# A decoder block in one core: up weights' low parts by an adding DMA, RNN work spread, one product moved

## The chip, the cores and the metric

The kernel runs on one core of one Trainium2 chip. The metric is the device time of an execution in microseconds (us). The core has a matrix engine (TensorE, PE in the rows; its weight loads are PEld), a vector engine (VectorE, DVE), an activation engine (ScalarE, ACT), a general engine (GpSimd, POOL) and a queue that issues transfers (SyncE, SP). Sixteen DMA engines move data between memory (HBM) and the on-chip memory (SBUF). TensorE accumulates in eight PSUM banks of 128 x 512 floats. Its clock has two levels, 2.4 and 1.2 GHz; the rows give the granted clock as a share of the higher one.

## What is computed

One decoder block over 512 tokens of width 1024, all in float32: a sparse attention with a top-k index, and a gated linear recurrence (RG-LRU), merged; then a convolutional feed-forward part. Cut to what matters here:

```
h  = cumulative recurrence of (a, x * i * sqrt(1 - a^2)) over the tokens   # 1024 channels
rnn = h * gelu(yr)
q, k, v, qi, ki, ... = split(rms_norm(x) @ w_in)       # attention over the 128 keys of best index score
h  = x + ga1 * (merge(attention, rnn) @ w_out)
up = causal_conv3(rms_norm(h) @ w_up)                  # 1024 -> 2 x 2816
val, gte = split(up)
h  = h + ga2 * ((silu(gte) * val) @ w_down)            # 2816 -> 1024
return rms_norm(h)
```

## The kernel before

**Three products for one.** Every float32 operand of a large product is split into a high part, rounded to the type that TensorE multiplies at full rate (fp32r), and a low part, the rest. A product is then three matmuls: high x high, high x low, low x high (`mm3`). For weights `split` (line 550) makes them: ScalarE copies the raw tile into the high part `wh`, VectorE subtracts that from the raw tile into the low part `wl`. `wtile` (line 755) loads the raw weights, one 1 MB DMA for two tiles of 128 output columns, and calls `split`.

**A planner sets the order.** The code records operations in `Plan.op` (line 199) with a planned cost, the engines that may run it, and its buffers; `Plan.order` (line 241) then simulates the engines, picks operations by a due time (`rank`) and writes out one fixed order for each engine. `P.fix` gives TensorE's work its planned time, `P.soft` gives an operation a due time, `P.hor` says how long before its due time it may take a buffer (`HORIZON` for most). Buffers are rings: `W` three raw weight tiles of 1 MB, `w` six split tiles, thus three pairs of high and low part, `t` 75 tiles of 128 x 512, `b` eight PSUM banks. In hardware each engine runs its list in order, so what waits holds up what stands behind it.

**The stages.** First the input projections by tiles (`xr`, `yr`, `qi`, `kw`, `k`, `v`, `q`, the gates). In between run the recurrent branch in two batches of four 128-channel blocks (`rnn_batch`, line 820), the index scores and the top-k loops on VectorE, and the attention. In `rnn_batch` the last part does for each block `m = sqrt(m)`, `u = u * m`, the scan `h`, `y = gelu(y)` and `y = y * h`; the due times are `at(RB[3])` and `at(RB[4])`, the same for all four blocks. Then come the output projections and the norm of the second half.

**The feed-forward part.** 44 up tiles follow (`up`, line 1213; tiles 2f and 2f+1 are the value and gate half of f tile f, 22 of them). An up tile is 8 x 3 matmuls of 512 columns. ScalarE takes its bank out into `cv`, VectorE adds two more convolution taps, and after each second tile comes the SiLU and the product with the other half, `acts[f]`. The down projection of f tiles 0 to 15 is done by one level of Strassen: seven products in place of eight (`product`, line 1177), each once over pairs 0 to 3 and once over pairs 4 to 7; the second round of seven is placed behind the up tiles named in `SPREAD[1]`, and each product's two banks are added into `total`. F tiles 16 to 21 go the plain way in the tail (line 1269 on): for every row block of 128 tokens (`ROWS` = 2, 3, 0, 1) and half of the columns six f tiles of three matmuls into one bank, then sum, norm and output. Their split weights are `dh`, `dl`, their split activations `acth`, `actl`.

Of the kernel before, what the change touches and what calls it, by code (L numbers as in the profile page):

```python
# [19 lines left out]
TT = S // 128  # L20
# [23 lines left out]
INFLATE = 1.03  # L44
HORIZON = 26
EARLY = 3
PAIRS = 8
ORDER = [[4, 3, 0, 2, 1, 5, 6], [0, 1, 2, 3, 4, 5, 6]]
ROWS = [2, 3, 0, 1]
SLICES = [(0, 4), (4, 8)]  # L50
SPREAD = [[17, 19, 21, 23, 25, 27, 29], [32, 34, 36, 37, 39, 41, 42]]
OUTS = [("wr", (0, 1, 2, 3)), ("wa", (0, 1)), ("wr", (4, 5)), ("wa", (2, 3, 4, 5, 6, 7)), ("wr", (6, 7))]
ADA0 = 28
COLD = 8.0
RBIAS = [14.0, 46.0, 48.0]
WARM = 12
DOT1 = 13.24
SECOND = -23.6
LATER = 13.94
CLOCK = 9.79  # L60
RB = [3.28, 6.04, 7.96, 11.0, 13.85, 0.61]
SOON = [20.91, 19.0, 21.69, 11.19]
ISTEP = {1: 14.0, 2: 38.5, 3: 93.3}
IW = {1: 18, 2: 49.4, 3: 51.9}
ASTEP = {0: 76, 1: 99.0, 2: 126, 3: 145}
AW = [8.6, 6.1, 18.7, 30.4]
BUMP = [0.01, 0.81]

# [96 lines left out]
class Op:  # L165
    __slots__ = ("engs", "emit", "reads", "writes", "deps", "succ", "rank", "idx", "func", "ready", "left",
                 "fixed", "soft", "hor", "after", "weak", "allocs", "lat", "end", "bufs", "start", "eng", "n", "tag", "shares")

# [8 lines left out]
class Plan:  # L177
# [20 lines left out]

    def op(self, engs, reads, writes, emit, func=None, hold=(), n=1, tag="", follow=None):
        o = Op()  # L200
        o.engs, o.emit, o.func = engs, emit, func
        o.n, o.tag = n, tag
# [38 lines left out]
    def order(self):  # L241
        ops = self.ops
        for o in reversed(ops):
            cost = min(o.engs.values())
            late = 1e9
            for s in o.succ:
                late = min(late, s.rank - 0.25 - cost * INFLATE)
            if o.fixed is not None:
                late = o.fixed
            if o.soft is not None:  # L250
                late = min(late, o.soft)
            o.rank = late
# [91 lines left out]
        while len(out) < n:  # L344
# [37 lines left out]
            for b in o.bufs:  # L382
                b.left -= 1
                b.end = max(b.end, o.end)
                if b.left == 0 and b.kind in SLOTS:
                    frees[b.kind].append(b.end + 0.1)
            for s in o.succ:
                s.left -= 1
                s.ready = max(s.ready, t if o in s.weak else o.end + max(LAT[e][x] for x in s.engs))
                if s.left == 0:  # L390
                    for x in s.engs:
                        avail[x].append(s)
# [7 lines left out]
def block_kernel(ctx: ExitStack, tc: tile.TileContext, x, cols, wada1, wada2, win0, win, wgate,  # L400
# [13 lines left out]
    def buf(kind, shape, dtype, name, reserve=0):  # L414
        uid[0] += 1
        return Buf(kind, shape, dtype, f"{name}_{uid[0]}", reserve)
# [338 lines left out]
    def wtile(src, c, sub, nk):  # L755
        key = (id(src), c)
        if key not in raws:
            raws[key] = buf("W", (128, nk, 256), F32, "wr")
            dma(raws[key], src[c], 128 * nk * 256 * 4)
        hi, lo = buf("w", (128, nk, 128), F32R, "wh"), buf("w", (128, nk, 128), F32R, "wl")  # L760
        split(hi, lo, raws[key][:, :, sub * 128:(sub + 1) * 128])
        return hi, lo
# [57 lines left out]
    def rnn_batch(js):  # L820
# [19 lines left out]
        for j in js:  # L840
# [9 lines left out]
            am[j] = (a, m)  # L850
        for j in js:
            a, m = am[j]
            u = g[j, 1]
            at(RB[3])
            act(m, m, AF.Sqrt)
            tt(u, u, m, ALU.mult, ("dve", "pool"))
            h = t2(name="h")
# [3 lines left out]
            at(RB[4])  # L861
            act(y, y, AF.Gelu_apprx_tanh)
            tt(y, y, h, ALU.mult, ("dve", "pool"))
            P.soft, P.hor = None, 20.0
# [403 lines left out]

    full = slice(0, 512)
    for t in ROWS:  # L1270
        parts, outs = [], []
        c = slice(t * 128, (t + 1) * 128)
        for h in range(2):
            cut = (t, h) == (ROWS[-1], 1)
            for n in [slice(0, 256), slice(256, 512)] if cut else [full]:
                ps = bank()
                for f in range(tail, FT):
                    hi, lo = dsplit[f, h]
                    planned(3 * pass_us(n.stop - n.start))
                    mm3(ps[:, n], asplit[f][0][:, c], asplit[f][1][:, c], hi[:, n], lo[:, n], f == tail, f == FT - 1)  # L1280
                    P.fix = None
                P.soft = clock[0] + 1.0
                v = total[t, h][:, n]
                tt(v, ps[:, n], v, ALU.add)
                o = t2(name="o")
                parts.append(v)
                outs.append((o, n, h))
                P.soft = clock[0] + 2.5
                tt(o[:, n], v, gfin[h][:, n], ALU.mult)
                P.soft = None  # L1290
        P.soft = clock[0] + 1.0
# [52 lines left out]
def _layout(i):  # L1344
# [25 lines left out]
    o["w_out"] = i["w_out"][0].reshape(4, 2, 128, 1024).transpose(0, 2, 1, 3)  # L1370
    o["w_up"] = _chunk(i["w_up"][0][:, ffo], 256)
    o["w_down"] = i["w_down"][0].reshape(11, 2, 128, 1024).transpose(0, 2, 1, 3)
# [26 lines left out]
```

## Time and profile before

| | |
|---|---|
| time, median of 3 runs | 787.84 us (786.66 to 787.93) |
| the profiled execution's own time | 790.1 us |
| its span, first to last instruction | 788.3 us |
| TensorE busy, matmuls | 768.4 us, 3579 |
| VectorE busy | 666.9 us |
| ScalarE busy | 461.4 us |
| GpSimd busy | 50.5 us |
| moved by the DMA queues | 126.22 MB |
| mean granted TensorE clock | 0.992 |

Busy time of TensorE is modelled from starts: matmuls overlap, so the distance between two starts says more than the length of one. "Idle before" is time in which the engine did nothing, with what ended it behind an arrow. Of a DMA the issue is seen on the queue of the engine that issues it, and its landing as the time until its semaphore.

### The profile page before, as it was taken

Reading aid. Unit: us, or ns where it says so; the run is one execution under the profiler, and the core shown is the slowest. Engines: PE = TensorE matmul, PEld = TensorE weight load, DVE = VectorE, ACT = ScalarE, POOL = GpSimd, SP = SyncE. Lnnn points to the kernel's source line nnn. Section 1 sums busy time; section 2 is a strip of 40 time slices with the busy share of each in tenths; the row PEclk is TensorE's granted clock in tenths of the full one; section 3 lists DMA queues with packets and bytes.
Section 4 is the critical chain, followed back from the end, with each engine's and each line's share of the span. In section 5 each row is a group of like instructions: output and inputs, shape, how many; then the busy total and the mean of one; then the engine's idle time right before and its main releaser. Section 6 shows DMA issues by size and latency. Waiting matters only on the chain.

```text
span 788.3 us, 10204 instructions
## 1 busy us (share of the span) xinstructions
PE 768.4 (97%) x3579; PEld 639.7 (81%) x3579; DVE 666.9 (85%) x1315; ACT 461.4 (59%) x815; POOL 50.5 (6%) x72
## 2 busy tenths in 40 slices
PE   7999999999899999999999999999999999999986
PEld 6888888887788887888789988888888888888865
DVE  6996976999999988869885867897977889997973
ACT  6589935599599779723335643665534454443522
POOL 1000000034021141000000000000000000000000
PEclk9999999999899999999999999999999999999999
DMA  9973132231121351648671343456445544676202
GB/s 342 404 276 111 54 128 85 81 133 54 54 107 55 133 187 55 223 163 312 242 274 39 134 178 116 160 193 209 160 160 199 176 178 155 217 247 201 98 27 81
DMA packets 35411, 126.22 MB, mean 160 GB/s; under 512 B 3944, under 2 KB 6432, under 8 KB 25504
## 3 DMA queue, kind: packets, MB, share of 16 engines
q1 hardware_dynamic: 35360, 125.58, 44.8%
q8 instruction: 28, 0.46, 0.2%
q14 instruction: 23, 0.19, 0.1%
HBM read 121.35 MB, written 5.79 MB: 161 GB/s over the span
## 4 chain that ended last, share of the span: by engine, by line
PE 54%; DVE 24%; DMA 12%; issue 4%; ACT 4%; SPq 0%; POOLq 0%; POOL 0%; DVEq 0%; ACTq 0%
PE ps L534 53%; DMA wd<-in_w_down_dram 7%; DVE dl L470 3%; DMA wr<-in_w_up_dram 3%; DVE wl L470 3%; DVE sum L470 3%; DVE cv L475 2%; DVE wd L470 2%; DVE wa L621 2%; DMA wa<-in_wada_dram 2%; PE ps L546 2%; ACT wh L463 1%; DMA wo<-in_w_out_dram 1%; DVE ahl L470 1%; DVE sc L901 1%
## 5 line engine op out<-in xcount | busy, mean ns | idle before, releaser
L534 PE MATMUL ps<-yl,wh 128*128 128x512 f32 (+1 forms) x376 | 141.7, 377 | 0.1
L534 PE MATMUL ps<-yh,wh 128*128 128x512 f32 (+1 forms) x376 | 141.4, 376 | 0.0
L534 PE MATMUL ps<-yh,wl 128*128 128x512 f32 (+1 forms) x376 | 141.2, 375 | 0.0
L463 ACT ACTIVATE wh<-wr 128x1024 fp32r<-128x1024 f32 (+1 forms) x96 | 97.7, 1019 | 59.6 <-PE ps L534 40.9
L470 DVE TENSOR_TENSOR wl<-wr,wh 128x1024 fp32r<-128x1024 f32 (+1 forms) x96 | 112.9, 1176 | 17.5 <-ACT wh L463 17.1
L534 PE MATMUL ps<-xh,wh 128*128 128x512 f32 x288 | 114.0, 396 | 0.0
L534 PE MATMUL ps<-xh,wl 128*128 128x512 f32 x288 | 113.2, 393 | 0.4 <-DVE wl L470 0.4
L534 PE MATMUL ps<-xl,wh 128*128 128x512 f32 x288 | 113.1, 393 | 0.0
L463 ACT ACTIVATE dh<-wd 128x512 fp32r<-128x512 f32 x68 | 42.5, 630 | 78.0 <-DVE wd L470 69.9
L534 PEld LDWEIGHTS ps<-yl,wh 128*128 128x128 f32 x376 | 70.7, 188 | 13.3 <-DVE yl L470 0.5
L534 PEld LDWEIGHTS ps<-yh,wl 128*128 128x128 f32 x376 | 70.7, 188 | 12.9
L534 PEld LDWEIGHTS ps<-yh,wh 128*128 128x128 f32 x376 | 70.7, 188 | 12.8
L475 DVE SCALAR_TENSOR_TENSOR cv<-ps,ct,cv 128x511 f32<-128x511 f32 x88 | 65.6, 745 | 11.9 <-ACT cv L463 11.2
L534 PE MATMUL ps<-dh,ahl 128*128 128x512 f32 x224 | 71.3, 389 | 0.0
L534 PEld LDWEIGHTS ps<-xh,wl 128*128 128x128 f32 x288 | 54.6, 189 | 12.7 <-DVE wl L470 1.2
L534 PEld LDWEIGHTS ps<-xl,wh 128*128 128x128 f32 x288 | 54.7, 190 | 10.3
L534 PEld LDWEIGHTS ps<-xh,wh 128*128 128x128 f32 x288 | 54.7, 190 | 10.2
L621 DVE SCALAR_TENSOR_TENSOR wa<-wa,crow 128x1024 f32<-128x1024 f32 x48 | 58.5, 1235 | 2.2 <-DMA wa<-in_wada_dram 2.2
L534 PEld LDWEIGHTS ps<-dh,ahl 128*128 128x128 f32 x224 | 42.0, 188 | 8.7
L470 DVE TENSOR_TENSOR dl<-wd,dh 128x512 fp32r<-128x512 f32 x68 | 45.8, 684 | 3.4 <-ACT dh L463 3.1
L463 ACT ACTIVATE cv<-ps,ct 128x512 f32<-128x512 f32 x44 | 33.7, 766 | 17.9 <-PE ps L534 17.9
L534 PE MATMUL ps<-dl,ahl 128*128 128x512 f32 x112 | 43.6, 389 | 0.0
(256 smaller groups left out, 1483.9 us busy)
## 6 DMA issues: line engine op xcount, KB each, us to landing
wa<-in_wada_dram SPq DMA_DIRECT2D x24, 1024.0 KB, 4.8
wd<-in_w_down_dram SPq DMA_DIRECT2D x96, 256.0 KB, 3.4
wr<-in_w_up_dram SPq DMA_DIRECT2D x22, 1024.0 KB, 5.0
wr<-in_win_dram SPq DMA_DIRECT2D x18, 1024.0 KB, 4.8
wr<-in_wo_rnn_dram SPq DMA_DIRECT2D x4, 1024.0 KB, 4.7
wo<-in_w_out_dram SPq DMA_DIRECT2D x4, 1024.0 KB, 4.9
wd<-in_w_down_dram SPq DMA_DIRECT2D x3, 1024.0 KB, 4.9
x<-in_x_dram SPq DMA_DIRECT2D x4, 512.0 KB, 9.6
```

The source lines that it names most:

```text
L463: nc.scalar.activation(real(dst), real(src), func, **kw)
L470: lambda e: ENG[e].tensor_tensor(real(dst), real(a), real(b), op=op), tag="tt")
L475: lambda e: nc.vector.scalar_tensor_tensor(real(dst), real(a), real(s), real(b), op0=op0, op1=op1), tag="stt")
L534: nc.tensor.matmul(real(ps), real(a), real(b), start=st, stop=sp)
L546: nc.tensor.transpose(real(ps[:, i * 128:(i + 1) * 128]), real(s), real(ident))
L621: vop(1.14, [r, crow], [r, dst], lambda: nc.vector.scalar_tensor_tensor(real(r), real(r), 1.0, real(crow), op0=ALU.mult, op1=ALU.mult, acc ...
L901: vop(0.125 + 0.00104 * W, [a, m8], [a], lambda m8=m8: nc.vector.match_replace(real(a), real(m8), real(a), TAKEN))
```

## The change

It has four parts.

1. In `wtile`, for up tiles from number 6 on (38 of the 44), the low part is no longer made by VectorE. ScalarE writes the high part, and in a second pass, with scale -1, the negated high part into the buffer of the low part. Then a DMA issued by GpSimd reads the raw weights of that tile once more from memory and adds them to it. The planner gives it 1.0 us on GpSimd and 3.0 us more until its result is there (`extra`). The layout of `w_up` in memory changes so that a tile's 512 KB are 4 KB a partition in one piece; the 1 MB load of two tiles stays.
2. In `rnn_batch` the u x m products and scans, and the y x h products, have due times of their own: a start (14.0 us behind the first batch's base, 24.7 behind the second's) plus 9.1 or 10.0 us for each further block, and 3.0 more for y x h.
3. The second round of products is placed behind other up tiles, the last one behind tile 43, the last of all, in place of tile 42. In the tail the first row block does f tiles 16 to 19 for both halves before f tiles 20 and 21.
4. The planner's constants: `HORIZON` 41 in place of 26, costs of ScalarE, VectorE and GpSimd 5% higher, and other due times.

```diff
-HORIZON = 26
+HORIZON = 41
+FIRST = 6
-SPREAD = [[17, 19, 21, 23, 25, 27, 29], [32, 34, 36, 37, 39, 41, 42]]
+SPREAD = [[17, 19, 21, 23, 25, 27, 28], [32, 33, 36, 38, 39, 42, 43]]
+SLACK = {"act": 1.05, "dve": 1.05, "pool": 1.05}
-DOT1 = 13.24
-SECOND = -23.6
-LATER = 13.94
-CLOCK = 9.79
-RB = [3.28, 6.04, 7.96, 11.0, 13.85, 0.61]
-SOON = [20.91, 19.0, 21.69, 11.19]
-ISTEP = {1: 14.0, 2: 38.5, 3: 93.3}
-IW = {1: 18, 2: 49.4, 3: 51.9}
-ASTEP = {0: 76, 1: 99.0, 2: 126, 3: 145}
-AW = [8.6, 6.1, 18.7, 30.4]
-BUMP = [0.01, 0.81]
+DOT1 = 14.92
+SECOND = -21.2
+LATER = 8.59
+CLOCK = 9.89
+RB = [3.28, 6.04, 7.96, 11.0, 15.86, 0.61]
+RNNV = [[14.0, 9.1], [24.7, 10.0]]
+SOON = [20.91, 19.0, 22.51, 13.74]
+ISTEP = {1: 14.0, 2: 38.1, 3: 91.6}
+IW = {1: 18, 2: 44.3, 3: 57.2}
+ASTEP = {0: 76, 1: 99.0, 2: 126, 3: 144.9}
+AW = [8.5, 7.3, 18.7, 32.4]
+BUMP = [0.01, 0.74]
...
-        o.engs, o.emit, o.func = engs, emit, func
+        o.extra = extra
+        o.engs = {e: c * SLACK.get(e, 1.0) for e, c in engs.items()}
+        o.emit, o.func = emit, func
...
     def wtile(src, c, sub, nk):
         key = (id(src), c)
         if key not in raws:
-            raws[key] = buf("W", (128, nk, 256), F32, "wr")
-            dma(raws[key], src[c], 128 * nk * 256 * 4)
+            if src is w_up:
+                raws[key] = buf("W", (128, 2, 1024), F32, "wr")
+                dma(raws[key], src[2 * c:2 * c + 2].rearrange("c p n -> p c n"), 1 << 20)
+            else:
+                raws[key] = buf("W", (128, nk, 256), F32, "wr")
+                dma(raws[key], src[c], 128 * nk * 256 * 4)
         hi, lo = buf("w", (128, nk, 128), F32R, "wh"), buf("w", (128, nk, 128), F32R, "wl")
+        if src is w_up:
+            w = raws[key][:, sub, :]
+            flat = [View(b, b.box(), (lambda a: a.rearrange("p k n -> p (k n)"),)) for b in (hi, lo)]
+            if 2 * c + sub < FIRST:
+                split(*flat, w)
+                return hi, lo
+            act(flat[0], w, AF.Copy, hold=[lo])
+            act(flat[1], w, AF.Copy, scale=-1.0)
+            P.op({"pool": 1.0}, [lo], [lo], lambda e: nc.gpsimd.dma_start(
+                real(flat[1]), src[2 * c + sub], accum_op=ALU.add), tag="acc", extra=3.0)
+            return hi, lo
         split(hi, lo, raws[key][:, :, sub * 128:(sub + 1) * 128])
         return hi, lo
...
             act(m, m, AF.Sqrt)
+            P.soft, P.hor = base + RNNV[js[0] // 4][0] + RNNV[js[0] // 4][1] * i, 20.0
             tt(u, u, m, ALU.mult, ("dve", "pool"))
...
             act(y, y, AF.Gelu_apprx_tanh)
+            P.soft, P.hor = base + RNNV[js[0] // 4][0] + RNNV[js[0] // 4][1] * i + 3.0, 20.0
             tt(y, y, h, ALU.mult, ("dve", "pool"))
...
+    def last(ps, t, h, n, f0, f1):
+        c = slice(t * 128, (t + 1) * 128)
+        for f in range(f0, f1):
+            hi, lo = dsplit[f, h]
+            planned(3 * pass_us(n.stop - n.start))
+            mm3(ps[:, n], asplit[f][0][:, c], asplit[f][1][:, c], hi[:, n], lo[:, n], f == tail, f == FT - 1)
+            P.fix = None
+
+    for i, t in enumerate(ROWS):
+        cuts = [(0, slice(0, 512)), (1, slice(0, 512))]
+        if i == TT - 1:
+            cuts = [(0, slice(0, 512)), (1, slice(0, 256)), (1, slice(256, 512))]
         parts, outs = [], []
...
+        banks = [bank() for _ in cuts]
+        if i == 0:
+            for ps, (h, n) in zip(banks, cuts):
+                last(ps, t, h, n, tail, FT - 2)
+        for ps, (h, n) in zip(banks, cuts):
+            last(ps, t, h, n, FT - 2 if i == 0 else tail, FT)
...
-    o["w_up"] = _chunk(i["w_up"][0][:, ffo], 256)
+    o["w_up"] = _chunk(i["w_up"][0][:, ffo], 128).reshape(2 * FT, 128, 1024)
```

## Rows read from the trace of the kernel before

**Rows 1.** The page, busy us (share of the span) and instructions of each engine:

```profile
PE 768.4 (97%) x3579; PEld 639.7 (81%) x3579; DVE 666.9 (85%) x1315; ACT 461.4 (59%) x815; POOL 50.5 (6%) x72
```

**Rows 2.** Stretches, busy us: PE, PEld, DVE, ACT, POOL; PEclk, DMA share, GB/s:

```profile
140.00:300.00 160.00, 156.22 (x719) 129.24 (x718) 155.28 (x368) 129.35 (x238) 41.30 (x50) 0.98 0.29 103
...
195.40:205.80 10.40, 7.03 (x22) 5.20 (x21) 10.08 (x24) 4.13 (x10) 1.84 (x2) 0.67 0.00 0
...
749.20:758.70 9.50, 6.01 (x17) 3.90 (x16) 9.30 (x17) 2.68 (x6) 0.00 (x0) 0.82 0.00 0
437.00:743.00 306.00, 306.00 (x1378) 254.44 (x1377) 263.88 (x439) 150.49 (x243) 0.00 (x0) 1.00 0.52 179
```

**Rows 3.** Timeline of TensorE, 195 to 209 us: start, us, instruction [idle before]:

```profile
195.42 0.22 PE L534 MATMUL ps<-kh,q 128*128 128x128 f32 x1
...
197.76 0.30 PE L534 MATMUL ps<-kh,q 128*128 128x128 f32 x1 [2.01 <-DVE q L475]
...
205.81 0.39 PE L534 MATMUL ps<-xh,wl 128*128 128x512 f32 x1
...
208.08 0.22 PE L534 MATMUL ps<-kh,q 128*128 128x128 f32 x1
...
208.25 0.45 PE L534 MATMUL ps<-xh,wh 128*128 128x512 f32 x1
```

**Rows 4.** Timeline of VectorE, 185 to 200 us, like operations merged:

```profile
185.30 3.02 DVE L470 TENSOR_TENSOR rg<-rg,m 128x512 f32<-128x512 f32 x4
188.25 5.23 DVE L858 TENSOR_TENSOR_SCAN h<-a,rg 128x512 f32<-128x512 f32 x4
193.40 2.97 DVE L470 TENSOR_TENSOR yr<-yr,h 128x512 f32<-128x512 f32 x4
...
196.87 3.09 DVE L475 SCALAR_TENSOR_TENSOR q<-ps,ct,q 64x512 fp32r<-64x512 f32 x4
```

**Rows 5.** Timeline of TensorE, 742 to 759 us:

```profile
742.86 0.39 PE L534 MATMUL ps<-yh,wl 128*128 128x512 f32 x1
743.08 0.39 PE L534 MATMUL ps<-dh,acth 128*128 128x512 f32 x1
...
750.75 0.40 PE L534 MATMUL ps<-dh,actl 128*128 128x512 f32 x1
754.10 0.50 PE L534 MATMUL ps<-dh,acth 128*128 128x512 f32 x1 [2.95 <-ACT acth L463]
...
759.00 0.40 PE L534 MATMUL ps<-dh,actl 128*128 128x512 f32 x1
```

**Rows 6.** Timeline of ScalarE, 747 to 754 us:

```profile
747.89 0.76 ACT L463 ACTIVATE cv<-ps,ct 128x512 f32<-128x512 f32 x1
751.67 0.63 ACT L463 ACTIVATE cv<-cv 128x512 f32<-128x512 f32 x1 [3.02 <-DVE cv L475]
753.41 0.63 ACT L463 ACTIVATE acth<-cv 128x512 fp32r<-128x512 f32 x1 [1.11 <-DVE cv L470]
```

**Rows 7.** Groups by line: count | busy us, mean ns | idle before, releasers:

```profile
L470 DVE TENSOR_TENSOR wl<-wr,wh 128x1024 fp32r<-128x1024 f32 x88 | 107.4, 1220 | 17.3 <-ACT wh L463 17.1
L463 ACT ACTIVATE wh<-wr 128x1024 fp32r<-128x1024 f32 x88 | 92.7, 1054 | 48.4 <-PE ps L534 29.8 <-DMA wr<-in_w_up_dram 16.1 <-issue 1.6
```

**Rows 8.** Timeline, up tile 16: high part begun, first matmul:

```profile
504.63 1.05 ACT L463 ACTIVATE wh<-wr 128x1024 fp32r<-128x1024 f32 x1
...
514.45 0.39 PE L534 MATMUL ps<-yh,wh 128*128 128x512 f32 x1
```

**Rows 9.** DMA issues: count, KB each, median us from issue to landing:

```profile
wr<-in_w_up_dram SPq DMA_DIRECT2D x22, 1024.0 KB, 5.0
...
x<-in_x_dram SPq DMA_DIRECT2D x4, 512.0 KB, 9.6
...
wr<-in_wo_attn_dram SPq DMA_DIRECT2D x4, 512.0 KB, 4.0
```

**Rows 10.** One tile's instructions: duration min/median/max ns, first and last start:

```profile
L534 PE MATMUL ps<-rh,wh x64: 387/389/481, 302.9 to 376.9; 128*128 128x512 f32 x64
```

More of the change, by code (lines that the diff above doesn't have):

```diff
@@ L166 @@
     __slots__ = ("engs", "emit", "reads", "writes", "deps", "succ", "rank", "idx", "func", "ready", "left",
-                 "fixed", "soft", "hor", "after", "weak", "allocs", "lat", "end", "bufs", "start", "eng", "n", "tag", "shares")
+                 "fixed", "soft", "hor", "after", "weak", "allocs", "lat", "end", "bufs", "start", "eng", "n", "tag", "shares", "extra")
 LAT = {"pe": {"pe": 0.0, "act": 0.2, "dve": 0.2, "pool": 0.2, "sp": 0.2},
@@ L197, in shares_port, with op @@
         return out
-    def op(self, engs, reads, writes, emit, func=None, hold=(), n=1, tag="", follow=None):
+    def op(self, engs, reads, writes, emit, func=None, hold=(), n=1, tag="", follow=None, extra=0.0):
         o = Op()
-        o.engs, o.emit, o.func = engs, emit, func
+        o.extra = extra
+        o.engs = {e: c * SLACK.get(e, 1.0) for e, c in engs.items()}
+        o.emit, o.func = emit, func
         o.n, o.tag = n, tag
@@ L243, in order @@
         for o in reversed(ops):
-            cost = min(o.engs.values())
+            cost = min(o.engs.values()) + o.extra
             late = 1e9
@@ L383, in order @@
                 b.left -= 1
-                b.end = max(b.end, o.end)
+                b.end = max(b.end, o.end + o.extra)
                 if b.left == 0 and b.kind in SLOTS:
@@ L388, in order @@
                 s.left -= 1
-                s.ready = max(s.ready, t if o in s.weak else o.end + max(LAT[e][x] for x in s.engs))
+                s.ready = max(s.ready, t if o in s.weak else o.end + o.extra + max(LAT[e][x] for x in s.engs))
                 if s.left == 0:
@@ L850, in rnn_batch @@
             am[j] = (a, m)
-        for j in js:
+        for i, j in enumerate(js):
             a, m = am[j]
@@ L1267, in block_kernel @@
             tt(v, v, back, ALU.add)
-    full = slice(0, 512)
-    for t in ROWS:
-        parts, outs = [], []
[L1272 to L1290, printed above, removed]
+    def last(ps, t, h, n, f0, f1):
[9 more added lines that the diff above has]
+            cuts = [(0, slice(0, 512)), (1, slice(0, 256)), (1, slice(256, 512))]
+        parts, outs = [], []
+        banks = [bank() for _ in cuts]
[4 more added lines that the diff above has]
+            last(ps, t, h, n, FT - 2 if i == 0 else tail, FT)
+            P.soft = clock[0] + 1.0
+            v = total[t, h][:, n]
+            tt(v, ps[:, n], v, ALU.add)
+            o = t2(name="o")
+            parts.append(v)
+            outs.append((o, n, h))
+            P.soft = clock[0] + 2.5
+            tt(o[:, n], v, gfin[h][:, n], ALU.mult)
+            P.soft = None
         P.soft = clock[0] + 1.0
```

## The prediction

> **What bounds the kernel now.** First the page: TensorE is busy 97% of the span [rows 1]. Then the table by stretches: from 437 to 743 us, nearly the whole stage of the up tiles and the Strassen products, TensorE has no idle time at all, at granted clock 1.00 [rows 2]. There nothing but TensorE's own work counts; VectorE (263.9 of 306 us busy) and ScalarE (150.5) are behind it. So the change, which takes no matmul away, can win only where TensorE stops. I looked for neighbouring 512-column matmuls that start further apart than the usual 0.227 us (24 of them are an up tile, 5.44 us). Two places are large.
>
> Stall A, 195.4 to 205.8 us: clock 0.67 [rows 2]. TensorE begins the q x k products at 195.42, waits 2.01 us for VectorE's `q`, once more for the next half, and is back at full pace at 205.81 [rows 3]. In those 10.39 us start 10 narrow and 11 wide matmuls (the 22 of the window's row less one begun before it). A narrow pair takes 0.17 us at full pace (208.08 to 208.25), so the work is 5 x 0.17 + 11 x 0.227 = 3.35 us: 7.0 us are lost, part as waits, part because the matmuls behind the waits run at the lower of the two clock levels, 1.2 GHz, until 205.81. Why `q` is late: VectorE runs twelve operations of the recurrent branch in a row from 185.30 on, 3.02 + 5.23 + 2.97 us, and only then the four halves of `q` at 196.87 [rows 4].
>
> Stall B, 749.2 to 759.0 us, clock 0.82 [rows 2]: in 9.80 us start 17 wide matmuls, 3.86 us of work, so 5.9 us are lost. TensorE waits 2.95 us for `acth`, the last up tile's result, and is at full pace again at 759.00 [rows 5]. That tile's last matmul starts at 742.86, yet `acth` is begun at 753.41: ScalarE takes the bank out at 747.89 only, and then waits 3.02 us for VectorE [rows 6], which is busy 9.30 of 9.50 us there [rows 2]. TensorE's cover were the tail's products that don't need that tile, 743.08 to 750.75 [rows 5]: 34 matmuls, 7.7 us.
>
> The rest (the start, small gaps, the work behind the last matmul) the change doesn't aim at.
>
> **The change, part by part.** (1) Weights. Of 44 up tiles 38 lose VectorE's subtraction, 1.22 us each: 46 us off VectorE. ScalarE gains a second pass over 1024 columns for each, 38 x 1.05 = 40 us [rows 7]. Over the 306 us VectorE falls from 264 to about 218, ScalarE rises from 150 to about 190: neither becomes the bound. TensorE doesn't wait there today, so by itself this is worth 0. What it could cost is the new chain: two passes on ScalarE, an issue on GpSimd's queue, a DMA that reads 512 KB from memory and adds it to what lies in SBUF, and its landing before the tile's third matmul. Nothing stands behind the waiting issue on GpSimd, which has no work at all from 437 to 743 us [rows 2]; its next are the norms of the tail. The tightest place is the run of tiles 6 to 17, with no product between them: there are three pairs of weight buffers, so ScalarE can begin a tile only when the tile three before it is done. The least time of the twelve is tile 16's: ScalarE starts at 504.63, TensorE at 514.45 [rows 8], 9.8 us, less 2.1 for the two passes: 7.7 us. The others leave 7.9 or 8.8, the tiles behind 17 leave 11 or more. No row shows a DMA that GpSimd issues or that adds. Nearest: 512 KB of attention weights land after 4.0 us, 1 MB of up weights after 5.0, the 512 KB pieces of `x` in the crowded start after 9.6 [rows 9]. I take 5 to 6, since it is one more 512 KB load beside middling traffic, with a second read: hidden, price 0. The end at 9.6 would cost (9.6 + 2.1 + 5.44 + 0.2) / 3 = 5.78 us a tile, 0.34 x 12 = 4 us; a gain on TensorE is excluded, since it has no idle time there to give back. The transfers themselves: 179 GB/s took a DMA share of 0.52 [rows 2], that is 2.9 us of all sixteen engines a MB, so half a MB takes 1.45, or 2.9 if the second read counts in full. 38 of them add 55 to 110 us to those 306: the share goes to 0.70 or 0.88, below 1. SP's own loads may land later; the same cushions cover that.
>
> The Trainium skill speaks of the adding itself ("Collectives: The Full Stack", The bandwidth ceiling): a reduction in the DMA engines reads two sources and runs at about half the rate of a copy. No trace here shows it; by it the upper share would hold, and the sum would stay as it is.
>
> (2) Recurrent branch. The u x m products, scans and y x h of each half get due times 9 to 10 us apart instead of a common one. No work is added or removed. The twelve operations no longer stand in one block before `q`, so stall A should go. Their 11.2 us of VectorE then lie between about 197 and 232 us, where VectorE is full too (155.28 of 160 us busy from 140 to 300 [rows 2]); work of the top-k loops and the attention comes forward in exchange. I take 6.0 of the 7.0 us and leave 1.0 as small waits. Bounds: 7.0 gained, or 0 if another result comes late in its place. What they feed is first read by TensorE at 302.9 [rows 10], some 70 us later: no wait there.
>
> (3) The end. The last product (four pairs, 24 matmuls, 5.44 us) moves behind the last up tile, and the first tail row does its four older f tiles for both halves before the last two. Cover for the last tile's chain: 7.7 us before, 7.7 + 5.44 = 13.1 after, against the 11.2 us it took (742.86 to 754.10). VectorE should also come there with less arrears, though the moved product's sums now fall into the same microseconds; they go into rows 0 and 1, which come last in the tail. I take 5.3 of 5.9 us; bounds 5.9, or 0 if the chain slips by as much as the cover grows.
>
> (4) Constants. A longer horizon, 5% slack on planned costs, due times shifted: they reorder everything by a little. Price 0, between -2 (TensorE's idle bits between 140 and 300, 160 less 156.22, hardly exceed stall A's) and +3, half of a stall like A.
>
> Sum against the profiled execution, 790.1 us (span 788.3 and 1.8 around it): 790.1 - 6.0 - 5.3 = 778.8. That execution lies 2.3 us above the median of the runs shown, 787.84, so the forecast for the median is **776.5**.
>
> **Rivals.** *A late landing (slower).* If it is L us from ScalarE's second pass to the landing, tiles 6 to 17 come every (L + 2.1 + 5.44 + 0.2) / 3 us. TensorE begins to stall at L of 7.7 to 8.8, and the loss eats the 11.3 us gained at 6.38 us a tile, L = 11.4. At L = 14 it is 7.25 us, 1.8 x 12 = 22 us: 798. For it: nothing shows such a DMA, `x` took 9.6 in the crowd, and if it cost three times a plain one the share would be 0.52 + 0.54, above 1. Against: the traffic in that run is below the start's.
>
> *GpSimd held off by VectorE.* Were issues let through only when VectorE pauses, a run of five operations of 1.22 us, the longest kind there [rows 7], on top of 5 to 6 us would make L about 12: (12 + 7.74) / 3 = 6.58, 1.14 x 12 = 14 us lost, 790. Waiting for one operation alone stays inside the cushion. The Trainium skill has a rule of this kind that speaks against the change ("SBUF — State Buffer", SBUF: two separate sides): the descriptors of a DMA from GpSimd's queue cannot be written while VectorE runs an operation in its two-port mode. The same page (Who interferes with whom) counts copies, casts and tensor-scalar as such and says that tensor-tensor has no such mode; VectorE's weight rows are tensor-tensor. No run so far shows the rule at work.
>
> *Stall A moves.* If the spread operations push the attention's back instead, stall B's gain is left and perhaps part of A's: 780 to 782.5.
>
> *Stall B stays.* If the product's own preparation and sums keep ScalarE's and VectorE's queues as long as before, the part does not do what it says and only A is gained: about 782.
>
> **How the numbers follow.** Forecast 0.62 (772.5 to 780), A moves 0.13, B stays 0.09, late landing 0.11, GpSimd held off 0.05. Measurement of this kernel tells about 0.2% (1.6 us) from no change. Faster: the first three less 0.02 for both stalls coming back, 0.82. The two DMA rivals start near break-even, so 0.03 of them and those 0.02 are within 0.2%: 0.05. Slower: 0.13. The lower end takes all of A and B (13 us) and 2 us of small gaps, 772.5, with 0.05 beyond; the upper end, 787, leaves 0.13 of late landings beyond.
>
> **What would show it.** Right: TensorE's starts 0.227 us apart through 185 to 235 us and the last 50 us, clock 1.00 in both; VectorE near 218 us over the up stage; adding DMAs that land within 7.7 us; `acth` of the last tile ready before TensorE asks. Wrong: TensorE waiting for `wl` between tiles 6 and 17, with a clock below 1; a new wait for VectorE between 200 and 330 us; a stall behind the last up tile.

## The result and the profile after

The changed kernel takes **837.67 us** (median of 4 runs, 834.62 to 840.56) where the kernel before, beside it on the same chip, takes 787.88: ratio **1.063** (95% interval 1.059 to 1.067). The forecast of 776.5 and its range, which ended at 787, were wrong by sign.

The page, queues and issues of the changed kernel (profiled execution 838.46 us, span 836.7). Columns: busy us (share of the span) and instructions of each engine; packets, MB, share of 16 engines; count, KB each, median us to landing:

```profile
PE 785.4 (94%) x3579; PEld 647.5 (77%) x3579; DVE 622.4 (74%) x1266; ACT 494.7 (59%) x852; POOL 102.2 (12%) x121
...
q1 hardware_dynamic: 38176, 125.58, 42.7%
q0 software_dynamic: 5472, 19.93, 13.4%
...
wd<-in_w_down_dram SPq DMA_DIRECT2D x96, 256.0 KB, 4.7
wr<-in_w_up_dram SPq DMA_DIRECT2D x22, 1024.0 KB, 5.4
wl<-in_w_up_dram POOLq DMA_DIRECT2D x38, 512.0 KB, 7.1
```

Against [rows 1] VectorE has 44.5 us less and ScalarE 33.3 us more, near the 46 and 40 that the change counts. TensorE's 785.4 is 17 us more for the same 3579 matmuls: part of them ran at the lower clock. Its stretches (PE, PEld, DVE, ACT, POOL; PEclk, DMA share, GB/s):

```profile
190.00:210.00 20.00, 20.00 (x100) 16.84 (x99) 18.53 (x51) 16.95 (x32) 6.66 (x7) 1.00 0.15 53
437.00:540.00 103.00, 102.85 (x453) 84.38 (x452) 62.32 (x124) 64.59 (x98) 13.87 (x16) 1.00 0.86 222
540.00:680.00 140.00, 118.05 (x469) 92.93 (x468) 79.77 (x138) 67.07 (x104) 12.44 (x15) 0.93 0.74 202
540.00:790.00 250.00, 216.40 (x878) 171.90 (x876) 150.25 (x259) 114.08 (x176) 19.42 (x23) 0.94 0.73 204
780.00:810.00 30.00, 23.86 (x77) 16.66 (x76) 28.10 (x49) 11.93 (x21) 0.56 (x1) 0.77 0.20 78
```

Stall A is gone: TensorE has no idle time from 190 to 210 us. The run of up tiles 6 to 17, where the forecast saw the danger, is nearly whole (102.85 of 103). The loss begins behind it, among the Strassen products: in 540 to 680, where before lay inside the stretch without idle time [rows 2], 469 matmuls start; at one per 0.227 us there is room for 617, so some 34 us are lost. Going by the starts of neighbouring matmuls, as the prediction did, 61 us are lost behind 540 (before: the 5.9 of stall B): 34 by 670, 14 between 710 and 770, 13 between 780 and 810. That is 55 more than before; less 6.3 at stall A it is 48.7, and the span grew by 48.4.

What TensorE and the others wait for from 540 us on (us in total, times, longest), for TensorE, then VectorE, then SP's queue; the last two lines are VectorE and SP's queue in the kernel before:

```profile
PE ps L539 <- DMA wl<-in_w_up_dram: 20.2, 8, 5.3
PE ps L539 <- DVE dl L475: 14.8, 9, 4.8
PE ps L539 <- ACT dh L468: 3.0, 3, 1.7
...
DVE wd L475 <- DMA wd<-in_w_down_dram: 78.6, 30, 6.5
...
SPq L454 <- DVE dl L475: 101.8, 36, 8.2
SPq L454 <- DMA wd<-in_w_down_dram: 64.7, 23, 8.9
...
DVE wd L470 <- DMA wd<-in_w_down_dram: 10.7, 12, 1.7
...
SPq L449 <- DVE dl L470: 72.2, 29, 6.5
```

The loads of down weights from 540 to 790 us, before and after (count, KB each, median us to landing):

```profile
wd<-in_w_down_dram SPq DMA_DIRECT2D x76, 256.0 KB, 3.4
...
wd<-in_w_down_dram SPq DMA_DIRECT2D x80, 256.0 KB, 4.4
```

TensorE's waits add up to 38 us; the other 23 of the 61 lie mostly in matmuls that start 0.43 us apart behind the waits, at 1.2 GHz (granted clock 0.50 from 562 to 566 us). The new low parts (`wl`) are half of the waits. The other half has to do with no up tile: it is the down weights of the products (`dl`, `dh`), and behind these VectorE waits 78.6 us for SP's plain loads (before: 10.7). One place in full, SP, VectorE, ScalarE, GpSimd, TensorE in turn (start, us, instruction [idle before]; SP's row of eight is a run of issues, four to 539.4 and four from 550.4 on):

```profile
537.59 14.92 SPq L454 DMA_DIRECT2D wd<-in_w_down_dram  x8
561.53 0.38 SPq L454 DMA_DIRECT2D wr<-in_w_up_dram  x1
...
544.82 0.69 DVE L475 TENSOR_TENSOR wd<-wd 128x512 f32<-128x512 f32 x1 [3.33 <-DMA wd<-in_w_down_dram]
548.47 0.69 DVE L475 TENSOR_TENSOR wd<-wd 128x512 f32<-128x512 f32 x1 [2.29 <-DMA wd<-in_w_down_dram]
...
549.74 0.68 DVE L475 TENSOR_TENSOR dl<-wd,dh 128x512 fp32r<-128x512 f32 x1
...
560.21 0.69 DVE L475 TENSOR_TENSOR wd<-wd 128x512 f32<-128x512 f32 x1 [4.11 <-DMA wd<-in_w_down_dram]
560.82 0.69 DVE L475 TENSOR_TENSOR dl<-wd,dh 128x512 fp32r<-128x512 f32 x1
...
545.54 0.63 ACT L468 ACTIVATE dh<-wd 128x512 fp32r<-128x512 f32 x1 [3.94 <-DVE wd L475]
546.08 1.04 ACT L468 ACTIVATE wh<-wr 128x1024 fp32r<-128x1024 f32 x1
549.19 0.63 ACT L468 ACTIVATE dh<-wd 128x512 fp32r<-128x512 f32 x1 [2.08 <-DVE wd L475]
549.73 1.04 ACT L468 ACTIVATE wl<-wr 128x1024 fp32r<-128x1024 f32 x1
...
555.54 0.63 ACT L468 ACTIVATE dh<-wd 128x512 fp32r<-128x512 f32 x1 [2.76 <-DVE wd L475]
...
551.07 0.87 POOL L778 DMA_DIRECT2D wl<-in_w_up_dram  x1 [10.85 <-ACT wl L468]
...
547.87 0.50 PE L539 MATMUL ps<-yh,wl 128*128 128x512 f32 x1 [1.96 <-DMA wl<-in_w_up_dram]
561.56 0.80 PE L539 MATMUL ps<-dl,ahl 128*128 128x512 f32 x1 [4.85 <-DVE dl L475]
```

Between its fourth and its fifth load SP issues nothing for 11 us: the three 1 MB slots of the raw weights (W) are taken. The fifth goes out at 550.45, when the `dl` of 549.74, the first pair's last reader, is done. That `dl` could have run at 546.2, behind its `dh`; in VectorE's fixed order it stands behind the second pair's `wd` (548.47), which combines that pair's two raw tiles and waited for their loads. So a late load also holds the slot of the pair before it. TensorE's wait until 561.56 is of the same kind: it needs the third pair's low part, whose `dh` was done at 556.17, but its `dl` (560.82) stands behind the `wd` of the fourth pair, which is complete only at 560.2. From 540 to 760 us low parts whose `dh` was done stood 23 us, in nine places, behind a `wd` that waited for a load; before it was 0.4 us. ScalarE works in order too: `dh`, which waits for the same loads, holds the next tile's two passes apart (546.08 and 549.73), so the adding DMA is issued late as well. Theory: the adding transfers make SP's loads land later, and since only three slots are there to be refilled, a late landing comes back in the next issue.

### The profile page after: what moved, and what is told of

Same layout as the page of the kernel before. It is cut to its first block, busy times and chain, and to the rows that moved or that the text cites. A ratio compares the mean times of both kernels' runs of the same rounds, so it can differ in the third digit from the quotient of the medians.

```text
span 836.7 us, 10257 instructions
## 1 busy us (share of the span) xinstructions
PE 785.4 (94%) x3579; PEld 647.5 (77%) x3579; DVE 622.4 (74%) x1266; ACT 494.7 (59%) x852; POOL 102.2 (12%) x121
## 3 DMA queue, kind: packets, MB, share of 16 engines
q1 hardware_dynamic: 38176, 125.58, 42.7%
q0 software_dynamic: 5472, 19.93, 13.4%
## 4 chain that ended last, share of the span: by engine, by line
PE 57%; DMA 23%; DVE 11%; ACT 5%; issue 3%; SPq 1%; POOL 0%; POOLq 0%; DVEq 0%; ACTq 0%
PE ps L539 54%; DMA wd<-in_w_down_dram 20%; DVE dl L475 3%; PE ps L551 3%; DVE wd L475 2%; ACT wl L468 2%; DVE cv L480 2%; DVE sum L475 1%; ACT wh L468 1%; SPq L454 1%; DMA wo<-in_w_out_dram 1%; DMA x<-in_x_dram 1%; DMA wa<-in_wada_dram 1%; ACT dh L468 1%; ACT cv L468 1%
## 5 line engine op out<-in xcount | busy, mean ns | idle before, releaser
L539 PE MATMUL ps<-yh,wl 128*128 128x512 f32 (+1 forms) x376 | 145.3, 387 | 20.2 <-DMA wl<-in_w_up_dram 20.2
L539 PE MATMUL ps<-yh,wh 128*128 128x512 f32 (+1 forms) x376 | 144.8, 385 | 0.0
L539 PE MATMUL ps<-yl,wh 128*128 128x512 f32 (+1 forms) x376 | 144.5, 384 | 0.2
L468 ACT ACTIVATE dh<-wd 128x512 fp32r<-128x512 f32 x68 | 42.9, 631 | 133.7 <-DVE wd L475 116.9
L475 DVE TENSOR_TENSOR wd<-wd 128x512 f32<-128x512 f32 x40 | 27.7, 692 | 83.8 <-DMA wd<-in_w_down_dram 79.7
L539 PEld LDWEIGHTS ps<-yl,wh 128*128 128x128 f32 x376 | 72.7, 193 | 14.4 <-DVE yl L475 0.6
L539 PEld LDWEIGHTS ps<-yh,wh 128*128 128x128 f32 x376 | 72.7, 193 | 13.3
L480 DVE SCALAR_TENSOR_TENSOR cv<-ps,ct,cv 128x511 f32<-128x511 f32 (+1 forms) x88 | 65.4, 746 | 18.0 <-ACT cv L468 17.5
L539 PE MATMUL ps<-dh,ahl 128*128 128x512 f32 x224 | 75.1, 405 | 3.0 <-ACT dh L468 3.0
L475 DVE TENSOR_TENSOR wl<-wr,wh 128x1024 fp32r<-128x1024 f32 (+1 forms) x58 | 70.3, 1214 | 8.7 <-ACT wh L468 8.6
L778 POOL DMA_DIRECT2D wl<-in_w_up_dram x38 | 33.3, 876 | 307.6 <-ACT wl L468 298.6
L626 DVE SCALAR_TENSOR_TENSOR wa<-wa,crow 128x1024 f32<-128x1024 f32 x48 | 58.8, 1243 | 12.7 <-DMA wa<-in_wada_dram 12.6
L539 PEld LDWEIGHTS ps<-xl,wh 128*128 128x128 f32 x288 | 54.1, 188 | 10.3
L539 PEld LDWEIGHTS ps<-dh,ahl 128*128 128x128 f32 x224 | 44.0, 196 | 13.4 <-ACT dh L468 4.2
```

What stands on the lines that cost most here:

```text
L468: nc.scalar.activation(real(dst), real(src), func, **kw)
L475: lambda e: ENG[e].tensor_tensor(real(dst), real(a), real(b), op=op), tag="tt")
L480: lambda e: nc.vector.scalar_tensor_tensor(real(dst), real(a), real(s), real(b), op0=op0, op1=op1), tag="stt")
L539: nc.tensor.matmul(real(ps), real(a), real(b), start=st, stop=sp)
L626: vop(1.14, [r, crow], [r, dst], lambda: nc.vector.scalar_tensor_tensor(real(r), real(r), 1.0, real(crow), op0=ALU.mult, op1=ALU.mult, acc ...
L778: P.op({"pool": 1.0}, [lo], [lo], lambda e: nc.gpsimd.dma_start(real(flat[1]), src[2 * c + sub], accum_op=ALU.add), tag="acc", extra=3.0)
```

## The experiments

The kernel before was measured again beside each group of runs; its medians went from 787.9 to 791.1 us. Ratios are to the runs beside it, so differences in us between runs of two groups are uncertain by some 3 us. In the runs without the DMA, with the plain copy and with nobody waiting, each engine keeps the changed kernel's order; in the others the planner lays out a new one. Rivals to the theory ("traffic"): the adding DMA's own landing; the new order and constants.

**What of the DMA costs.** The DMA left out; the same DMA as a plain copy; the same transfers with nobody waiting for them; and, for the second stall further down, no adding DMA and no second ScalarE pass.

```
-    P.op({"pool": 1.0}, [lo], [lo], lambda e: nc.gpsimd.dma_start(..., accum_op=ALU.add), ...)
+    P.op({"pool": 1.0}, [lo], [lo], lambda e: None, ...)                                    # no add
+    ... nc.gpsimd.dma_start(real(flat[1]), src[2 * c + sub]) ...                             # plain copy
+    ... nc.gpsimd.dma_start(real(flat[1] if c < 9 else crow), ..., accum_op=ALU.add) ...     # spare tile
-FIRST = 6
+FIRST = 44                                                                                  # no adding DMA at all
```

> The changed kernel in its own order, but the 38 adding DMAs are not issued (the low parts stay the negated high parts, so the low part of these weights is left out). Everything else stays: the second ScalarE pass, the constants, the place of the products. Three theories for the 50 us lost. Traffic: an adding DMA holds the 16 DMA engines about twice as long for a byte as a plain one, so SP's raw weights land later, the three raw slots come free later, and everything behind them is late. Landing: the adding DMA itself lands 7 to 10 us after its issue where the order counts on 4, and the matmuls of its tile wait. Order: the new order, the constants or the second ScalarE pass lose the time, whatever the DMA does. Traffic and landing: 775 to 782 us (787.9 less the 11 us of the two stalls that this kernel no longer has). Order: 825 to 838.

Measured: 782.56 us, ratio 0.9925 (0.9891 to 0.9959), just above the range given, since its second stall costs 8 us. Order, constants and second pass don't lose the 50 us. VectorE waits here 32.7 us in 27 waits for `wd` from 540 us on, more than before, and yet TensorE has no idle time from 540 to 700:

```profile
DVE wd L475 <- DMA wd<-in_w_down_dram: 32.7, 27, 2.9
```

> The changed kernel, instruction for instruction, but the 38 DMAs of GpSimd copy the weights over the low part and don't add (so the low part is wrong: the sum with the negated high part is left out). Bytes, packets, issues and waits are the same. If what counts is that adding takes a DMA engine twice as long for a byte, the queue's time falls from 112 to about 57 us of 16 engines and its landing from 7.1 to about 4.5 us, and the kernel takes 778 to 795 us (traffic and landing both). If it is the 20 MB more of reads whatever is done with them: 825 to 838. Order: 825 to 838.

Measured: 811.28 us, ratio 1.028 (1.0245 to 1.0315), between the two expectations. Over the kernel without the DMA the plain copies cost 28.7 us and the adding 26.4 more. Its queue:

```profile
q0 software_dynamic: 5472, 19.93, 7.6%
```

That is 61 us of 16 engines for what took 112 when adding (13.4% of 836.7): 3.1 and 5.6 us a MB. SP's loads of down weights landed after 4.3 us in the median from 540 to 790 beside the copies and 4.4 beside the adding DMAs. The median doesn't tell the two apart; by what path the adding costs twice as much is not shown.

> The changed kernel, same order; from tile 18 on the adding DMAs are issued at the same place but add into a spare tile that nothing reads (the low parts of those tiles stay the negated high parts). The traffic is that of the changed kernel, and no matmul waits for it. Traffic: 820 to 838 us, with VectorE's waits for the wd loads as long as in the changed kernel (82 us). Landing: 775 to 785 us and those waits back at 13 to 30 us. A spare tile that is added to one DMA after the other may spread the issues by a few us. Order: 825 to 838.

Measured: 828.54 us, ratio 1.0499 (1.0464 to 1.0534). With no one waiting for the low parts of tiles 18 to 43 only 9.1 us come back. From 540 us on VectorE still waits for `wd` and TensorE for `dl`:

```profile
DVE wd L475 <- DMA wd<-in_w_down_dram: 64.9, 29, 6.8
...
PE ps L539 <- DVE dl L475: 14.0, 10, 4.7
```

Half of TensorE's waits named `wl`; without these 44 of the 61 us behind 540 are still lost by the starts. The 17 less are what the landing cost there at most; 7.6 us are lost anew from 437 to 540, 2.6 of them in a wait for the low part of tile 17. So traffic is the larger part, and landing not nothing.

> The changed kernel, but the program that lays out the order is told 8.0 us for an adding DMA where it was told 4.0 (measured: 7.1 at the middle, 10.5 at most). If only the landing itself were the loss, 785 to 800 us. If the traffic is (the run with transfers that nobody waits for lost all but 9 us of it), at most those 9 us come back: 828 to 838 us; asking for the raw up weights sooner may hold a slot longer and give less.

Here `extra=7.0` stands for `extra=3.0`. Measured: 827.34 us, ratio 1.0469 (1.0413 to 1.0524): just under the range. An order that knows the landing gains 10.3 us (12.8 by the ratios), about the 9.1 of the run before, and leaves the rest. What SP's own loads now take the planner was not told in any run.

> The kernel before with the adding DMAs alone (second ScalarE pass, joined loads of the up weights), its constants, its RNN places and its order of products. If the DMAs lose the time whatever the rest does, 58 us over the kernel before less nothing: 840 to 850 us, with both stalls of the kernel before still in it. If it is the meeting of the DMAs with the new constants or the moved product: 788 to 800.

Its edit is the part of the change's diff in `wtile`, of `extra` and of the layout, on the kernel before. Measured: 848.58 us, ratio 1.0738 (1.0676 to 1.0799). The DMAs lose the time in the old order as well.

**Slots or a full DMA?** The raw down weights of the products go into the 128x512 tiles:

```
-            raw = buf("W", (128, len(rhs), 512), F32, "wd")
+            raw = [t2(name="wd") for _ in rhs]
...
```

> The changed kernel with all its adding DMAs; only the raw down weights of the Strassen products go into 128x512 tiles (of which there are 75) and no longer into the three 1 MB slots that they share with the raw up weights. The two runs with the transfers changed say that traffic carries most of the loss; this one asks how. Slots: the loads land later, so each of the three slots is held longer, and the next load can only be issued when one comes free; with more places for them the loads go out earlier and the later landing is hidden: 785 to 805 us (the 9 us that the landing of the adding DMA costs may stay), SP's waits for a free slot far under the 78 us of the changed kernel. Share: the 16 engines are too full for the loads, however early they are issued: 825 to 838.

Measured: 794.76 us, ratio 1.0061 (1.004 to 1.0081): 42.9 us come back with all 38 adding DMAs still there. Stretches; for 540 to 790, the issues; and what SP's queue waits for from 540 on:

```profile
437.00:540.00 103.00, 91.75 (x378) 74.23 (x378) 62.65 (x117) 59.43 (x87) 13.22 (x15) 0.93 0.91 257
540.00:680.00 140.00, 138.95 (x613) 114.70 (x613) 91.52 (x164) 78.74 (x128) 13.97 (x16) 1.00 0.82 225
...
wd<-in_w_down_dram SPq DMA_DIRECT2D x65, 256.0 KB, 7.9
wl<-in_w_up_dram POOLq DMA_DIRECT2D x23, 512.0 KB, 8.6
...
SPq L454 <- ACT wl L468: 74.1, 10, 13.9
...
SPq L454 <- DVE dl L475: 12.7, 3, 5.8
```

The clearest lines of the study: from 540 to 680 the DMA is fuller than in the changed kernel (0.82 against 0.74), the loads land later (7.9 us; 4.4 there), and TensorE loses 1 us where it lost 34. Lateness costs next to nothing when the loads are issued early enough; the slots forbade that. SP's wait for the down weights' slots falls from 101.8 to 12.7 us. It now waits 74.1 us for the up weights' slots, and nothing comes of it. The edit gives room to both kinds of load and a new order to VectorE, so what each adds, and whether an order with `dl` ahead of the next pair's `wd` would have helped with three slots, is not tested. What is left, 17.6 us, lies between 460 and 510: the products' loads now run ahead into the run of tiles 6 to 17 (DMA share 0.91), and there the new low parts come late (waits of TensorE for `wl` at 465, 478 and 505 us, 3.0, 4.9 and 3.4 us).

**Where the adding DMA does no harm.** Only tiles 6 to 17; only from tile 18 on, with the roomier raw weights:

```
-            if 2 * c + sub < FIRST:
+            if not FIRST <= 2 * c + sub < 18:          # only 6 to 17
-FIRST = 6
+FIRST = 18                                             # from 18 on, and the raw weights in 128x512 tiles
```

> The changed kernel with the adding DMA for tiles 6 to 17 only, where no product's loads run beside them; tiles 18 to 43 have their low parts from VectorE. If the transfers lose time only where they meet the loads of the products, this takes the time of the kernel without any adding DMA, 779.6 us, within 2; if each adding DMA costs its share (50 to 58 us over 38), 12 of 38 cost 16 to 18 us: 796 to 798.

Measured: 788.26 us, ratio 0.9984 (0.9955 to 1.0014). My expectation fell: 8.6 us over the kernel without adding DMAs. By the starts 8.1 us are lost from 437 to 540, in one stall, at tile 17:

```profile
503.55 0.63 ACT L468 ACTIVATE dh<-wd 128x512 fp32r<-128x512 f32 x1 [3.44 <-DVE wd L475]
...
505.76 1.04 ACT L468 ACTIVATE wl<-wr 128x1024 fp32r<-128x1024 f32 x1
...
507.10 0.87 POOL L778 DMA_DIRECT2D wl<-in_w_up_dram  x1 [8.38 <-ACT wl L468]
...
517.59 0.79 PE L539 MATMUL ps<-yh,wl 128*128 128x512 f32 x1 [5.09 <-DMA wl<-in_w_up_dram]
```

The products' weights are prepared long before their place in TensorE's order: a `dh` that waits 3.44 us stands ahead of tile 17's passes, and a landing of some 10 us does the rest. "No product between them" holds for TensorE, not for SP and ScalarE.

> The changed kernel with the raw down weights in 128x512 tiles, and the adding DMA for tiles 18 to 43 only. With all 38 of them, that kernel lost 17.6 us between 460 and 510 us and 1.3 us behind it. If the loss at 460 to 510 is the adding DMAs of tiles 6 to 17 meeting the loads of the products, which now run far ahead: 775 to 780 us. If it is those loads alone, or if the meeting moves to the first tiles behind 17: 785 to 795.

Measured: 778.27 us, ratio 0.9845 (0.9818 to 0.9872). 26 adding DMAs cost next to nothing once the slots are roomy and the run of up tiles is spared: TensorE loses 0.5 us at most behind 437 by the starts.

**The second stall.** Without any adding DMA, three slots (first); the products back; six adding DMAs; roomy raw weights; and these with six adding DMAs, on the kernel before, and with the products back:

```
-FIRST = 6
+FIRST = 44                                             # six adding DMAs: FIRST = 38
-SPREAD = [..., [32, 33, 36, 38, 39, 42, 43]]
+SPREAD = [..., [32, 33, 36, 38, 39, 41, 42]]           # products back
-            raw = buf("W", (128, len(rhs), 512), F32, "wd")
+            raw = [t2(name="wd") for _ in rhs]         # roomy raw weights
...
```

> The changed kernel with FIRST = 44: all low parts by VectorE as before, no second ScalarE pass, no adding DMA; the spread RNN operations, the moved product, the constants and the joined loads of the up weights stay. If the two stalls were read rightly, 776.5 us (6.0 and 5.3 us less than before), between 774 and 780, with TensorE busy through 195 to 206 and less than 1 us idle around 745 to 755. Traffic and landing say the same. Order (the constants or the new places lose the time): 820 and more.

Measured: 779.64 us, ratio 0.9877 (0.9855 to 0.9899), inside the range, but the stall behind the last up tile is still there:

```profile
740.86 0.50 PE L539 MATMUL ps<-dl,acth 128*128 128x512 f32 x1 [1.75 <-DVE dl L475]
...
743.26 0.80 PE L539 MATMUL ps<-dl,acth 128*128 128x512 f32 x1 [1.43 <-DVE dl L475]
```

It costs 5.3 us with the lower clock behind it (5.9 before). TensorE no longer waits for the last up tile's `acth` but for `dl`, low parts of the tail's weights, from a VectorE that has no pause there.

> The changed kernel without any adding DMA (FIRST = 44), and the last two products back behind tiles 41 and 42 where the kernel before has them. If moving the last product behind the last up tile shortens the second stall by some 5 us as forecast, this kernel takes 784 to 786 us; if the stall only moves, 779 to 781 us as with the product moved.

Measured: 777.19 us, ratio 0.9828 (0.98 to 0.9856), below both ranges, and the stall is 2.4 us: moving the product was no gain; here it is nearer to a loss, though the two intervals just touch.

> The changed kernel with the adding DMA for tiles 38 to 43 only, raw weights in the three slots: 6 low parts, about 7 us, are taken off VectorE just ahead of the second stall, and 3 MB of adding transfers are put on the queues there. VectorE as the cause of the second stall: it shrinks from 5.3 to under 2 us, 775 to 777 us. Slots: the stall stays or grows, 779 to 788 us (6 of 38 shares of the loss of 58 us are 9 us).

Measured: 796.41 us, ratio 1.0068 (1.004 to 1.0096), above both ranges. Taking 7 us of work off VectorE made the stall 13 us long, with 7 us more lost just ahead of it. So it is not VectorE's capacity.

> The changed kernel without any adding DMA (FIRST = 44) and with the raw down weights of the products in 128x512 tiles. In the run without adding DMAs the second stall stayed (5.3 us of TensorE around 738 to 746 us), while in the run with all of them but roomier raw weights it was gone. Slots: the stall comes from raw weights that wait for a slot and pile up VectorE's work at the end; then it goes here: 774 to 776 us. VectorE: the stall is VectorE's own load of sums and low parts, lighter only where the DMA took over the low parts; then nothing changes: 779 to 781 us.

Measured: **775.96 us**, ratio 0.9818 (0.9792 to 0.9844), no stall: the fastest median of the study, ahead of both kernels. The last two stretches, without adding DMAs and with three slots:

```profile
700.00:735.00 35.00, 35.00 (x156) 29.00 (x155) 30.92 (x48) 15.30 (x23) 0.00 (x0) 1.00 0.53 181
735.00:762.00 27.00, 23.82 (x98) 18.70 (x97) 25.24 (x46) 10.65 (x21) 1.09 (x2) 0.94 0.11 39
```

The same stretches with six adding DMAs and three slots:

```profile
700.00:735.00 35.00, 29.91 (x123) 23.91 (x123) 21.08 (x34) 11.85 (x17) 1.73 (x2) 0.95 0.73 196
735.00:762.00 27.00, 20.11 (x68) 13.32 (x67) 24.36 (x41) 11.28 (x19) 0.00 (x0) 0.86 0.28 109
```

And without adding DMAs, with roomy raw weights:

```profile
700.00:735.00 35.00, 35.00 (x156) 28.97 (x156) 33.69 (x56) 16.25 (x28) 0.00 (x0) 1.00 0.27 91
735.00:762.00 27.00, 27.00 (x121) 22.37 (x120) 19.20 (x37) 6.47 (x16) 1.65 (x3) 1.00 0.11 40
```

Read the third busy time, VectorE's. Where it gets through little work up to 735 us (21.08 of 35; from 690 to 735 it stands 18.1 us for `wd`), the tail's work is left for the stretch behind, and TensorE waits there; where raw weights have room it does 33.69 before and TensorE has all of its 27 us.

> The adding DMA for tiles 38 to 43 only, as in the run that took 796.4 us, and the raw down weights of the products in 128x512 tiles. If those 17 us were lost because VectorE stood idle for raw weights that had no slot and had its tail work left over afterwards: 776 to 779 us, and no stall behind 735 us. If the adding DMAs lose it by their own landing or by the engines they fill: 785 and more.

Measured: 776.09 us, ratio 0.9844 (0.9804 to 0.9884), no stall: the 17 us of the six adding DMAs went through the slots.

> The kernel before with nothing changed but the raw down weights of the products in 128x512 tiles. If the second stall of the kernel before (5.9 us) comes from raw weights that wait for one of three slots, it goes and the kernel is 4 to 6 us faster than before (ratio 0.992 to 0.995), with the first stall (7.0 us) still in it. If that stall is VectorE's load or the product's place: no change (ratio 0.998 to 1.002).

Measured: 785.06 us, ratio 0.9958 (0.9935 to 0.998), just above the range of the slots. Stall B is gone from the kernel before by that edit alone (735 to 762 us: TensorE busy 27.00 of 27, clock 1.00); 2.9 of its 5.9 us are lost again elsewhere, most in a wait for the output weights at 383 us that grew from 0.7 to 1.9 us, with its slower matmuls.

> The changed kernel without any adding DMA, with the raw down weights in 128x512 tiles, and the last two products back behind tiles 41 and 42. With three slots the place of the products moved the time by 2.4 us (779.6 and 777.2). If that came through the slots, there is nothing left to gain here: 775 to 776.5 us. If the place counts by itself: 773 to 774.5.

Measured: 776.43 us, ratio 0.9845 (0.9815 to 0.9875): with roomy slots the product's place is worth nothing that can be told.

## Why the prediction was wrong

**Step 1, the DMA at price 0, failed**, by some 58 us (837.67 less the 779.64 of the kernel without it; 55 of them for the DMA and 3 for ScalarE's second pass in place of VectorE's subtraction, by the 782.56 of the kernel that only leaves the DMA out). Its terms one by one:

- The landing, taken at 5 to 6 us, was 7.1 in the median, inside the bounds of 4.0 to 9.6, but 10.5 at most. That tiles 6 to 17 came through (102.85 of 103 us) is not the cushion of 7.7 us: counted as the prediction counts L, five of the twelve landings took longer, up to 9.5. The changed order left 9.3 us or more ahead of the third matmul of tiles 6 to 16, and tile 17, which had 7.0, had a landing of 6.9. That is luck: in the run with tiles 6 to 17 alone tile 17's took 10.7, and TensorE waited 5.09 us.
- The transfers were sized rightly: 55 to 110 us of 16 engines were given, 112 measured, and the share over the same stretch, 437 to 743, was 0.79, inside 0.70 to 0.88.
- The sentence that broke is "SP's own loads may land later; the same cushions cover that". The cushion was counted on the up tiles' weight buffers. The products' loads have none of it: they go through three slots, and a load that lands later is also the next load issued later. The trace of before showed the ring, and I didn't read it: from 540 us on SP's queue waits 72.2 us for `dl`, the last reader of a slot, so a load can't go out earlier to make up for a later landing. VectorE's 12 short waits for `wd` alone (10.7 us) were no such sign: the kernel with the DMA left out has 27 of them, 32.7 us, and TensorE loses nothing up to 700.
- "A share below 1" was read as room. The kernel with roomy slots ran at 0.82 all but undisturbed, the changed one lost 34 us at 0.74: the share doesn't say it. Whether a load can be issued early enough does.

The rival of a late landing had the right sign and the wrong place: no stall in tiles 6 to 17 of the changed kernel, and its 798 us missed 40 us of the loss. Its stall shows in other runs (tile 17 above; 460 to 510 us with the roomy raw weights). GpSimd held off by VectorE didn't happen: the 38 issues took 863 to 1042 ns (median 872), and 37 times GpSimd's idle time before them ended with ScalarE's pass. The Trainium skill ("SBUF — State Buffer", Who interferes with whom) gives tensor-tensor operations no such mode; these issues agree, since the two that fell where VectorE was idle took 872 ns like the rest.

**Step 2, stall A, was right**: 6.3 us gained by the starts (6.0 forecast), TensorE busy 20.00 of 20 from 190 to 210 us in the changed kernel, and nothing took its place up to 330 us (from 210 us on 4.9 us of small losses in the kernel without adding DMAs, 6.5 before).

**Step 3, stall B, failed**: 0.6 us gained, in the kernel without adding DMAs, where 5.3 were forecast; the changed kernel lost 13 us there, from 780 to 810. The rival "stall B stays" was right (782 forecast, 779.6 measured). The cover grew as counted, and `acth` was no longer waited for; but the arithmetic took VectorE's arrears as given. They come from raw weights without a slot, and the moved product's weights and sums add to them, so `dl` was late instead.

**Step 4, the constants**: priced 0 between -2 and +3; of the 9.0 us less lost in the kernel without adding DMAs 6.3 are A and 0.6 B, which leaves a gain of 2.1. No run tells it apart from the noise.

Of the 61.2 us by which the forecast missed, step 1 is 58 and step 3 is 4.7; steps 2 and 4 give back 0.3 and 2.1, and 0.9 is left over.

## What to carry to other kernels

Before adding traffic to a stage whose bound engine has no idle time, look at the loads that already run there: who issues them, whether the issue waits for a slot or for nothing, and how long after landing their reader starts. Loads that wait for a slot can't be issued earlier when they land later, whatever the DMA share says; a reader's short waits by themselves are no sign either way, as the kernel with the DMA left out shows. An in-order engine hands lateness on: ScalarE held up the passes of the up tiles, and VectorE held finished pairs' low parts, and with them the slots, behind a `wd` whose loads were late. Room for loads in flight decided the outcome here: moving the raw weights to another pool took 43 us off the changed kernel, 3.7 off the one without adding DMAs and 2.8 off the kernel before. The adding DMA itself gained nothing in any run, since TensorE was the bound where it relieved VectorE.

## What the runs showed of the hardware

An adding DMA of 512 KB, issued by GpSimd, took 5.6 us of 16 engines a MB where the same DMA as a plain copy took 3.1 and SP's plain loads 2.8 (42.7% of 836.7 us for 125.58 MB), that is 1.8 times the copy. The Trainium skill's half rate for a reduction in the DMA engines ("Collectives: The Full Stack", The bandwidth ceiling) fits this within a tenth; I had weighed it as changing no term of the sum. Its landing in the stage of the products was 7.4 us in the median against 5.2 for the plain copy.

A second surprise is what the lower clock level added: of the 61 us lost behind 540, 38 were waits, and most of the other 23 were matmuls 0.43 us apart, at 1.2 GHz, behind them (granted clock 0.93 from 540 to 680 us, 0.77 from 780 to 810).
